# A decoder trunk in FP32: the depth of the weight splits in the first 20 blocks, vector prices in the planner, a margin for woven steps

## The chip, the cores and the metric

One core of a Trainium2 chip runs one launch. The metric is the device time of that launch in microseconds (us). Five engines work side by side: TensorE (PE in the profile; its weight loads are listed apart as PEld), VectorE (DVE), ScalarE (ACT), GpSimd (POOL) and SyncE (SP), which issues most DMAs. About 0.2% of the time is what a measurement of this kernel can tell from no change.

## What is computed

Two layers act on 512 prompt tokens and 8 x 4 sample tokens, 544 columns in all, in FP32. Each layer is a mixer (a retention part and a dilated attention part that read one projection) and a ConvFFN:

```python
x += W_out [ RetentionGroup(h) || DilatedAttnGroup(h) ],  h = RMSNorm(x)   # h @ W_in, 28 column blocks of 128
x += ConvFFN(RMSNorm(x))                # up-proj -> causal conv width 3 -> SiLU gate -> down-proj
```

The attention of the prompt is, for each head and each strip of 128 queries, `p = exp(s - m)`, `den = sum(p)`, `o = (p / den) @ v`. A final RMSNorm ends the trunk.

## The kernel before

**Products.** Each FP32 product is done as three FP32R products: a weight tile `raw` is split into a rounded part `wh` (ACT, a copy) and the rest `wl` (DVE, `raw - wh`; for `w_up` ACT and a GpSimd DMA that adds). The activations are split likewise into `xh` and `xl`. A main block is one column block of 128 outputs: for each of its 8 `k` (128 rows of the contraction) it issues 6 matmuls of 272 columns (3 products, 2 halves of the tokens) into a PSUM tile `ps`. These 6 are called a k-step here. Two `ps` tiles exist, so a block may start when the block before the last one has been read out (its "evacuation").

**Weight units.** `halves` lists the units of weights in the order of use; the blocks 0 and 1 have two units each (s = 0 to 3), then each block of `w_in` and `w_up` has one. `load_w(s)` issues the DMA of unit s on SP, `split_w(s)` issues `wh` on ACT at once and puts `wl` into the planner's list under the name "split". There are RAWS = 3 raw tiles and UNITS = 4 pairs of `wh` and `wl`. In the loop at line 1428 the block that uses unit s loads unit s + 4 when it starts and splits unit s + 3 in its middle.

**The start.** Blocks 0 and 1 run together (lines 1406 to 1423) before the first RMSNorm is known. The norm's sum of squares goes through PE into `sec`, then ACT and DVE make `rstd` from it (`var`, two `tmp`, `rstd` on DVE). Block 0's `ps` is copied to `ev` by ACT, and `va` on DVE is `ev` or `ps` times `rstd`. Block 3 can't start before block 1's `ps` has been read by its `va`. GpSimd multiplies the two rotary tables `rope` by `rstd` as soon as that exists.

**Woven work.** All other work is written as generators: attention units, retention heads, evacuations, splits. `Stream.pump`, called after each k-step, issues from them whatever the planner `Clock` thinks ready. `Clock` holds an estimated end for each tile; `Engine.charge` (line 126) prices each instruction. The order in which instructions stand in each engine's queue is set when the program is built, by these estimates alone; on the chip each queue runs in that order and waits on semaphores. A PE piece is issued when its inputs are estimated done MARGIN = 0.3 us before PE's estimated time.

**An attention unit** (`att_unit`, line 735) has two halves: scores on PE (`sec<-ka,qa`), bias and maximum on DVE (`p<-sec,cst`), exponential and sum on ACT, then on DVE a reciprocal of one column and a scale of the whole tile (`tensor_scalar`, in the profile `TENSOR_SCALAR p<-p,pm`, of 128 to 512 columns), then the transposes on PE (`sec<-cst,p`). There are 32 such halves in each layer's first 16 blocks, where the blocks' evacuations (`rotary_out`: `ra`, four `rb` on DVE, then two additions `ka` or `qa` on GpSimd) fall as well.

**Woven down-projection** (`Weave`). The first 16 of the 22 ConvFFN rows go through `w_down` in 4 groups by a scheme with 7 products where 8 would be needed. A group has 4 sets m of 7 steps (P1, P4, P6, P2, P5, P7, P3), 6 matmuls each into `sec`, put between the k-steps of the next group's blocks. `tick` counts k-steps: a step is issued when it is `ready`, or at the latest when the count forces it (line 622). The weights of a set are split into `ah`, `al` (DVE) and the sums `sh`, `sl` (DVE); P1 and P4 are the first to use `al`.

Of the kernel before, what the change touches and what calls it, by code (L numbers as in the profile page):

```python
# [27 lines left out]
STEPS = (("P1", 0, 0), ("P4", 0, 2), ("P6", 1, 1), ("P2", 0, 1), ("P5", 1, 0), ("P7", 1, 2), ("P3", 1, 3))  # L28

LEAD, AMONG = 24, 40  # L30
EPS = 1e-6
NEG = -1e30
BLK = 562
# [13 lines left out]
NCONV = 352  # L47
EARLY = 640
RAWS, UNITS = 3, 4


def ADDED(block):
# [52 lines left out]
class Engine:  # L105
# [20 lines left out]
    def charge(self, method, outs, ins, args, kw):  # L126
        c, kind = self.clock, self.kind
        n = free_size(outs[0]) if outs else 0
        if method == "dma_start" and kind == "pool":
            c.issue(kind, [], [*outs, *ins], 1.0)  # L130
            c.dma = max(c.dma, c.now["pool"] + 1.0) + n * outs[0].shape[0] * 4 / 1.8e5
            c.wrote[c.key(outs[0])] = ("sp", c.dma + 1.0)
            return
        if method == "dma_start":
            c.now["sp"] = max(c.now["sp"], c.when("sp", ins)) + 0.06
            c.dma = max(c.dma, c.now["sp"] + 0.8) + n * outs[0].shape[0] * 4 / 3.6e5
            c.wrote[c.key(outs[0])] = ("sp", c.dma + 1.0)
            return
        if kind == "pe":
            rows = outs[0].shape[0]  # L140
            if method == "transpose":
                cost = max(n, 128) * 2 / 2400
            elif (kw["lhsT"]).dtype == F32R:
                cost = max(n / 2400, 0.107)
            else:
                side = min(rows, kw["lhsT"].shape[0])
                cost = max(n * 4 / 2400, 0.21) / (1 if side > 64 else 128 // side)
            cost += 0.003
        elif kind == "act":
            ptr = sum(free_size(i) == 1 for i in ins[1:])  # L150
            cost = 1.3 if method.startswith("preload") else n / 1200 + 0.093 * (1 + ptr)
        elif kind == "dve":
            half = method in ("tensor_scalar", "tensor_copy")
            cost = (n * (0.5 if half else 1) + 66 + (60 if len(ins) > 2 else 0)) / 960
        else:
            cost = 0.1 + n * (2.2 if len(ins) > 1 else 1.0) / 1000
        c.issue(kind, outs, ins, cost)
# [84 lines left out]
def trunk(ctx: ExitStack, tc: tile.TileContext, xin, w_in, w_out, w_up, w_down, q_down, kc, vc, s0, sctx_d, params_d,  # L242
          consts_d, rope_d, y_o, kv_o, pret_o, sret_o, conv_o):
    nc = tc.nc
    clock = Clock()
    pe, act, dve, pool, sp = (Engine(clock, k, e) for k, e in (
        ("pe", nc.tensor), ("act", nc.scalar), ("dve", nc.vector), ("pool", nc.gpsimd), ("sp", nc.sync)))
# [59 lines left out]
    def done(n=1):  # L307
        st.banks += n
# [31 lines left out]
    def load_w(s):  # L340
        if s < len(halves):
            i, a, b = halves[s]
            if s < 4:
                raw[s] = blk([128, b - a, 128], F32, "raw")
            else:
                raw[s] = rotate(wpool.tile([128, b - a, 128], F32, name=name("raw"), tag="raw", bufs=RAWS), "raw",
                                RAWS)
            sp.dma_start(*weights_of(s, raw[s]))
# [52 lines left out]
    class Norm:  # L401
# [47 lines left out]
        def rsqrt(self, ps, shape):  # L449
# [6 lines left out]
            for c, p in enumerate(ps):  # L456
                dve.tensor_scalar(v[:, c], p[:, :HC], -0.5 / D, -0.5 * EPS, op0=OP.mult, op1=OP.add)
            done(len(ps))
# [142 lines left out]
    class Weave:  # L601
# [25 lines left out]
        def ready(self, m, p, g, q):  # L627
            if (m, g) not in self.weights or any(p not in self.forms(i) for i in range(self.nk)):
                return False
            aps = [*self.weights[m, g], *(t for i in range(self.nk) for t in self.forms(i)[p])]  # L630
            return clock.when("pe", aps) <= clock.now["pe"]

        def prepare(self):

# [771 lines left out]
    for k in range(KB):  # L1406
        if k == 2:
            load_w(5)
        if k == 4:
            split_w(4)  # L1410
            load_w(6)
        if k == 6:
            split_w(5)
            load_w(7)
        for n in range(2):
            s = 2 * n + k // 4
            products(main[n], ps[n], k, parts_of(s), k // 4 * 4)
            if k % 4 == 3:
                split.pop(s)
            if k == KB - 1:  # L1420
                main[n]["evac"](ps[n])
                ps[n] = None
            st.pump(0.7)
    sp.dma_start(cst[1], consts_d[:, EARLY:])
    sp.dma_start(taps, params_d[:, NPAR:])

    split_w(6)
    for i, b in enumerate(main[2:-KB]):
        st.block = i + 2
        if b["pre"]:  # L1430
            b["pre"]()
        ps = main_bank()
        for pi, (a, e) in enumerate(b["parts"]):
            s = b["first"] + pi
            at, count = b["at"], b["count"]
            if at == 0:
                load_w(s + 4)
                w = parts_of(s)
                split.pop(s)
            for k in range(a, e):  # L1440
                if 2 * (at * (e - a) + k - a) == count * (e - a):
                    split_w(s + 3)
                products(b, ps, k, w, a - at * (e - a))
                st.pump(0.7)
                if b["weave"]:
                    b["weave"].tick()
        b["evac"](ps)
        st.pump()
# [3 lines left out]
    for c in range(2):  # L1452
        for n, b in enumerate(main[-KB:]):
            s, nk = b["first"], b["nk"]
# [145 lines left out]
```

## Time and profile before

| what | value |
|---|---|
| time, median of 3 runs | 1438.18 us (1438.09 to 1438.63) |
| the profiled execution | 1439.3 us |
| its span, first to last instruction | 1437.5 us |
| mean granted TensorE clock | 0.993 |
| PE busy | 1407.0 us, 98% of the span |
| DVE, ACT, POOL busy | 68%, 46%, 32% |

The span is what the trace covers; 1.8 us of the profiled execution lie around it. Since PE is busy for 98% of the span, the views of interest are those that show PE's stops: the waits by engine, the timeline around a stop, and the stretches with the granted clock. A matmul's end is modelled, and matmuls overlap, so the distance from start to start of two matmuls tells more than their durations. All calls go through one helper, so every row has line L123, and the tiles' names tell the groups apart.

### The profile page before, as it was taken

Reading aid. Unit: us, or ns where it says so; the run is one execution under the profiler, and the core shown is the slowest. Engines: PE = TensorE matmul, PEld = TensorE weight load, DVE = VectorE, ACT = ScalarE, POOL = GpSimd, SP = SyncE. Lnnn points to the kernel's source line nnn. Section 1 sums busy time; section 2 is a strip of 40 time slices with the busy share of each in tenths; the row PEclk is TensorE's granted clock in tenths of the full one; section 3 lists DMA queues with packets and bytes.
Section 4 is the critical chain, followed back from the end, with each engine's and each line's share of the span. In section 5 each row is a group of like instructions: output and inputs, shape, how many; then the busy total and the mean of one; then the engine's idle time right before and its main releaser. Section 6 shows DMA issues by size and latency. Waiting matters only on the chain.

```text
span 1437.5 us, 28709 instructions
## 1 busy us (share of the span) xinstructions
PE 1407.0 (98%) x11442; PEld 1336.1 (93%) x11442; DVE 977.5 (68%) x1823; ACT 667.3 (46%) x1074; POOL 457.8 (32%) x833
## 2 busy tenths in 40 slices
PE   8999999999999999999999999999999999999997
PEld 7888878999999999999997888889999999999996
DVE  8767545576577777776777764455856786868665
ACT  5254223436555454554434452233666454645434
POOL 4312211102546455541022231110135464645303
PEclk8999999999999999999999999999999999999999
DMA  6224584348765656563331247733677566566522
GB/s 252 75 83 156 187 318 157 125 132 212 180 170 129 172 132 171 125 174 82 102 132 69 87 158 269 286 122 117 201 174 179 155 139 164 131 174 143 138 71 77
DMA packets 83494, 219.99 MB, mean 153 GB/s; under 512 B 8992, under 2 KB 13216, under 8 KB 83360
## 3 DMA queue, kind: packets, MB, share of 16 engines
q1 hardware_dynamic: 70688, 172.01, 34.7%
q0 software_dynamic: 12672, 46.14, 18.3%
q8 instruction: 90, 1.47, 0.4%
q14 instruction: 44, 0.36, 0.1%
HBM read 205.91 MB, written 12.21 MB: 152 GB/s over the span
## 4 chain that ended last, share of the span: by engine, by line
PE 81%; DVE 10%; POOL 4%; issue 3%; ACT 2%; DMA 0%; SPq 0%; DVEq 0%; ACTq 0%; POOLq 0%
PE ps L123 58%; PE sec L123 23%; DVE p L123 3%; DVE rb L123 2%; POOL fb L123 1%; POOL fa L123 1%; POOL sums L123 1%; DVE wl L123 1%; DVE c L123 1%; DVE ra L123 1%; ACT fh L123 1%; DVE lb L123 0%; DVE x L123 0%; ACT wh L123 0%; DVE al L123 0%
## 5 line engine op out<-in xcount | busy, mean ns | idle before, releaser
L123 PE MATMUL ps<-xh,wh 128*128 128x272 f32 x2304 | 491.1, 295 | 4.4 <-DVE va L123 3.5
L123 PE MATMUL ps<-xh,wl 128*128 128x272 f32 x2304 | 478.4, 289 | 1.5 <-DVE wl L123 1.4
L123 PE MATMUL ps<-xl,wh 128*128 128x272 f32 x2304 | 478.3, 289 | 0.0
L123 PEld LDWEIGHTS ps<-xh,wh 128*128 128x128 f32 x2304 | 361.6, 189 | 22.2 <-issue 19.2
L123 PEld LDWEIGHTS ps<-xh,wl 128*128 128x128 f32 x2304 | 363.0, 189 | 1.9 <-DVE wl L123 1.9
L123 PEld LDWEIGHTS ps<-xl,wh 128*128 128x128 f32 x2304 | 363.1, 189 | 0.1
L123 ACT ACTIVATE wh<-raw 128x1024 fp32r<-128x1024 f32 (+1 forms) x182 | 181.9, 1000 | 66.9 <-PE ps L123 54.6
L123 ACT ACTIVATE c<-u,taps 128x560 f32<-128x560 f32 x88 | 75.4, 857 | 238.4 <-DVE u L123 200.0
L123 POOL DMA_DIRECT2D wl<-w_up x88 | 76.8, 873 | 336.4 <-ACT wl L123 314.4
L123 DVE SCALAR_TENSOR_TENSOR c<-u,taps,c 128x560 f32<-128x560 f32 x176 | 150.6, 856 | 45.4 <-ACT c L123 41.9
L123 DVE TENSOR_TENSOR x<-x,sec 128x272 f32<-128x272 f32 (+1 forms) x224 | 105.9, 475 | 91.4 <-PE sec L123 89.8
L123 DVE TENSOR_TENSOR wl<-raw,wh 128x1024 fp32r<-128x1024 f32 (+1 forms) x94 | 108.0, 1151 | 13.7 <-ACT wh L123 11.1
L123 POOL COPY last<-u 128x2 f32<-128x2 f32 (+1 forms) x176 | 39.2, 260 | 176.2 <-DVE u L123 176.2
L123 ACT ACTIVATE wl<-wh 128x1024 fp32r<-128x1024 f32 x88 | 92.7, 1053 | 1.3
L123 DVE TENSOR_TENSOR u<-ps,rstd 128x512 f32<-128x512 f32 (+1 forms) x176 | 68.9, 433 | 35.0 <-PE ps L123 34.7
L123 DVE TENSOR_TENSOR rb<-ps,rope 32x544 f32<-32x544 f32 (+1 forms) x96 | 69.2, 721 | 1.4
L123 DVE TENSOR_TENSOR x<-x,ps 128x544 f32<-128x544 f32 (+1 forms) x72 | 46.9, 654 | 31.0 <-PE ps L123 30.9
L123 POOL TENSOR_TENSOR sums<-uraw 128x256 f32<-128x256 f32 x64 | 63.6, 995 | 10.2 <-DVE sl L123 10.2
L123 DVE CUSTOM_DVE_ANT_0 p<-sec,cst 128x128 f32<-128x128 f32 (+3 forms) x64 | 29.2, 489 | 53.1 <-PE sec L123 52.8
L123 POOL TENSOR_TENSOR kr<-ra,rb 128x512 f32<-128x512 f32 (+1 forms) x16 | 14.2, 911 | 151.0 <-DVE rb L123 69.4
L123 PE MATMUL sec<-fh,sl 128*128 128x272 f32 x192 | 55.4, 289 | 0.3 <-DVE sl L123 0.3
L123 PE MATMUL sec<-fl,sh 128*128 128x272 f32 x192 | 55.3, 288 | 0.0
(196 smaller groups left out, 2537.3 us busy)
## 6 DMA issues: line engine op xcount, KB each, us to landing
raw<-w_up SPq DMA_DIRECT2D x88, 512.0 KB, 4.5
wl<-w_up POOLq DMA_DIRECT2D x88, 512.0 KB, 5.6
raw<-w_in SPq DMA_DIRECT2D x54, 512.0 KB, 4.1
kt<-kc SPq DMA_DIRECT2D x80, 256.0 KB, 5.9
vt<-vc SPq DMA_DIRECT2D x80, 256.0 KB, 5.0
uraw<-q_down SPq DMA_DIRECT2D x32, 512.0 KB, 4.1
raw<-w_out SPq DMA_DIRECT2D x16, 512.0 KB, 3.7
s<-s SPq DMA_DIRECT2D x16, 256.0 KB, 6.0
```

Of the source, the lines that this page charges most:

```text
L123: return f(*args, **kw)
```

## The change

Three edits. In `charge`, DVE's `tensor_scalar` and `tensor_copy` are priced by all their columns, not half of them, and `tensor_scalar` and `reciprocal` get 0.09 us more. In `Weave.ready` a woven step counts as ready only when its operands are estimated done LATE = 1.0 us before PE's time (line 631). In the block loop the split goes two units ahead and the load three, up to block index i = 20, where both catch up by one unit (two loads and two splits in that block); the load of unit 7 in the opening loop and the split of unit 6 behind it fall away, since the loop does them now.

```diff
@@ -28,6 +28,8 @@
 STEPS = (("P1", 0, 0), ("P4", 0, 2), ("P6", 1, 1), ("P2", 0, 1), ("P5", 1, 0), ("P7", 1, 2), ("P3", 1, 3))
 
 LEAD, AMONG = 24, 40
+
+LATE = 1.0
 EPS = 1e-6
 NEG = -1e30
 BLK = 562
@@ -47,6 +49,7 @@
 NCONV = 352
 EARLY = 640
 RAWS, UNITS = 3, 4
+DEEPER = 20
 
 
 def ADDED(block):
@@ -150,8 +153,9 @@
             ptr = sum(free_size(i) == 1 for i in ins[1:])
             cost = 1.3 if method.startswith("preload") else n / 1200 + 0.093 * (1 + ptr)
         elif kind == "dve":
-            half = method in ("tensor_scalar", "tensor_copy")
-            cost = (n * (0.5 if half else 1) + 66 + (60 if len(ins) > 2 else 0)) / 960
+            cost = (n + 66 + (60 if len(ins) > 2 else 0)) / 960
+            if method in ("tensor_scalar", "reciprocal"):
+                cost += 0.09
         else:
             cost = 0.1 + n * (2.2 if len(ins) > 1 else 1.0) / 1000
         c.issue(kind, outs, ins, cost)
@@ -628,7 +632,7 @@
             if (m, g) not in self.weights or any(p not in self.forms(i) for i in range(self.nk)):
                 return False
             aps = [*self.weights[m, g], *(t for i in range(self.nk) for t in self.forms(i)[p])]
-            return clock.when("pe", aps) <= clock.now["pe"]
+            return clock.when("pe", aps) + LATE <= clock.now["pe"]
 
         def prepare(self):
 
@@ -1411,7 +1415,6 @@
             load_w(6)
         if k == 6:
             split_w(5)
-            load_w(7)
         for n in range(2):
             s = 2 * n + k // 4
             products(main[n], ps[n], k, parts_of(s), k // 4 * 4)
@@ -1424,7 +1427,7 @@
     sp.dma_start(cst[1], consts_d[:, EARLY:])
     sp.dma_start(taps, params_d[:, NPAR:])
 
-    split_w(6)
+    ahead = 2
     for i, b in enumerate(main[2:-KB]):
         st.block = i + 2
         if b["pre"]:
@@ -1434,12 +1437,17 @@
             s = b["first"] + pi
             at, count = b["at"], b["count"]
             if at == 0:
-                load_w(s + 4)
+                load_w(s + ahead + 1)
+                if i == DEEPER:
+                    ahead = 3
+                    load_w(s + ahead + 1)
                 w = parts_of(s)
                 split.pop(s)
             for k in range(a, e):
                 if 2 * (at * (e - a) + k - a) == count * (e - a):
-                    split_w(s + 3)
+                    if i == DEEPER:
+                        split_w(s + ahead - 1)
+                    split_w(s + ahead)
                 products(b, ps, k, w, a - at * (e - a))
                 st.pump(0.7)
                 if b["weave"]:
```

What the edits move, at three places. The numbers in the names are buffer numbers, which count differently in the two programs; the changed program's helper stands at line 126.

DVE at the start, from the estimate `tmp` of the first norm to the evacuation of block 1 (`va` from `ps_198`); `wl` are splits of weight units. Before:

```order
L123 TENSOR_TENSOR tmp_310<-rstd_308 128x544
L123 TENSOR_TENSOR tmp_310<-tmp_310,var_309 128x544
L123 TENSOR_TENSOR wl_326<-raw_252,wh_325 128x1024
L123 SCALAR_TENSOR_TENSOR rstd_308<-tmp_310,rstd_308 128x544
L123 TENSOR_TENSOR wl_360<-raw_281,wh_359 128x1024
L123 TENSOR_TENSOR va_377<-ev_302,rstd_308 128x512
L123 TENSOR_TENSOR va_377<-ev_302,rstd_308 128x32
L123 TENSOR_TENSOR va_380<-ps_198,rstd_308 128x512
L123 TENSOR_TENSOR va_380<-ps_198,rstd_308 128x32
```

And in the changed program:

```order
L126 TENSOR_TENSOR tmp_308<-rstd_306 128x544
L126 TENSOR_TENSOR tmp_308<-tmp_308,var_307 128x544
L126 SCALAR_TENSOR_TENSOR rstd_306<-tmp_308,rstd_306 128x544
L126 TENSOR_TENSOR va_364<-ev_300,rstd_306 128x512
L126 TENSOR_TENSOR va_364<-ev_300,rstd_306 128x32
L126 TENSOR_TENSOR va_367<-ps_198,rstd_306 128x512
L126 TENSOR_TENSOR va_367<-ps_198,rstd_306 128x32
L126 TENSOR_TENSOR wl_354<-raw_252,wh_353 128x1024
L126 TENSOR_TENSOR ra_392<-ps_323,rope_187 128x544
```

The two `wl` that stood before and behind `rstd` are gone from there: unit 6's stands behind the evacuation, unit 7's comes a block later.

DVE in layer 0, one attention unit of 256 columns (`p` from `sec` is the bias step, TENSOR_SCALAR the scale) and the evacuation of block 5 (`ra`, `rb`). Before:

```order
L123 ISA p_641,pm_642<-sec_637,cst_81 128x256
L123 ISA pm_642 128x1
L123 ISA p_644,pm_645<-sec_639,cst_81 128x256
L123 ISA pm_645 128x1
L123 TENSOR_TENSOR ra_648<-ps_567,rope_187 128x544
L123 TENSOR_TENSOR rb_649<-ps_567,rope_189 32x544 x4
L123 RECIPROCAL pm_642<-pm_642 128x1
L123 TENSOR_SCALAR p_641<-p_641,pm_642 128x256
L123 RECIPROCAL pm_645<-pm_645 128x1
L123 TENSOR_SCALAR p_644<-p_644,pm_645 128x256
```

And in the changed program:

```order
L126 TENSOR_TENSOR ra_624<-ps_561,rope_187 128x544
L126 TENSOR_TENSOR rb_625<-ps_561,rope_189 32x544 x4
L126 ISA p_679,pm_680<-sec_675,cst_81 128x256
L126 ISA pm_680 128x1
L126 ISA p_682,pm_683<-sec_677,cst_81 128x256
L126 ISA pm_683 128x1
L126 RECIPROCAL pm_680<-pm_680 128x1
L126 TENSOR_SCALAR p_679<-p_679,pm_680 128x256
L126 RECIPROCAL pm_683<-pm_683 128x1
L126 TENSOR_SCALAR p_682<-p_682,pm_683 128x256
```

The unit's scales stood right behind `rb` and now stand behind both bias steps, which follow `rb`.

PE at the first woven step of layer 0's second group (`sec` from `h`, `l` and `al`), among the k-steps of a block (`ps_5693`). Before:

```order
L123 MATMUL ps_5693<-xh_3762,wh_5481 128x272 x2
L123 MATMUL ps_5693<-xl_3777,wh_5481 128x272 x2
L123 MATMUL ps_5693<-xh_3762,wl_5482 128x272 x2
L123 MATMUL sec_5712<-h_883_5425,ah_5671 128x272
L123 MATMUL sec_5712<-l_884_5426,ah_5671 128x272
L123 MATMUL sec_5712<-h_883_5425,al_5672 128x272
```

And in the changed program:

```order
L126 MATMUL ps_5693<-xh_3762,wh_5481 128x272 x2
L126 MATMUL ps_5693<-xl_3777,wh_5481 128x272 x2
L126 MATMUL ps_5693<-xh_3762,wl_5482 128x272 x2
L126 MATMUL ps_5693<-xh_3820,wh_5481 128x272 x2
L126 MATMUL ps_5693<-xl_3834,wh_5481 128x272 x2
L126 MATMUL ps_5693<-xh_3820,wl_5482 128x272 x2
L126 MATMUL ps_5693<-xh_3850,wh_5481 128x272 x2
L126 MATMUL ps_5693<-xl_3861,wh_5481 128x272 x2
L126 MATMUL ps_5693<-xh_3850,wl_5482 128x272 x2
L126 MATMUL sec_5727<-h_883_5425,ah_5671 128x272
L126 MATMUL sec_5727<-l_884_5426,ah_5671 128x272
L126 MATMUL sec_5727<-h_883_5425,al_5672 128x272
```

The step stands two k-steps later; the first steps of the other three groups move by two, four and two k-steps in the same way, in both layers, and the last step of each group stays where it was.

## Rows read from the trace of the kernel before

**Rows 1.** The page: busy us (share of the span) xinstructions, engine by engine.

```profile
PE 1407.0 (98%) x11442; PEld 1336.1 (93%) x11442; DVE 977.5 (68%) x1823; ACT 667.3 (46%) x1074; POOL 457.8 (32%) x833
```

**Rows 2.** Waits of PE: waiter <- releaser: us in total, times, longest us.

```profile
PE sec L123 <- DVE p L123: 6.8, 8, 1.1
PE ps L123 <- DVE va L123: 3.5, 1, 3.5
PE sec L123 <- DVE al L123: 3.0, 6, 0.6
...
PE sec L123 <- DVE sl L123: 0.3, 2, 0.2
```

**Rows 3.** Waits of PE's weight loads, same columns.

```profile
PEld sec L123 <- DVE p L123: 6.9, 14, 1.0
```

**Rows 4.** Timeline at the start: start us, us, engine line op out<-in xcount [idle before].

```profile
27.19 1.22 DVE L123 TENSOR_TENSOR wl<-raw,wh 128x1024 fp32r<-128x1024 f32 x1
...
28.33 0.72 DVE L123 SCALAR_TENSOR_TENSOR rstd<-tmp,rstd 128x544 f32<-128x544 f32 x1
...
28.96 1.22 DVE L123 TENSOR_TENSOR wl<-raw,wh 128x1024 fp32r<-128x1024 f32 x1
...
29.18 3.93 POOL L123 TENSOR_TENSOR rope<-rope,rstd 128x544 f32<-128x544 f32 x2 [12.27 <-ACT wh L123]
...
30.10 3.06 DVE L123 TENSOR_TENSOR va<-ev,rstd 128x512 f32<-128x512 f32 x2
30.12 0.41 PE L123 MATMUL ps<-xh,wl 128*128 128x272 f32 x2
...
33.09 0.78 DVE L123 TENSOR_TENSOR va<-ps,rstd 128x512 f32<-128x512 f32 x2
...
34.01 0.79 PE L123 MATMUL ps<-xh,wh 128*128 128x272 f32 x2 [3.48 <-DVE va L123]
...
39.54 0.41 PE L123 MATMUL ps<-xh,wh 128*128 128x272 f32 x2
```

**Rows 5.** Stretches: us, busy us (x) of PE PEld DVE ACT POOL, PEclk, DMA, GB/s.

```profile
5.30:8.80 3.50, 2.29 (x12) 1.54 (x11) 2.55 (x4) 2.30 (x5) 2.17 (x2) 0.99 0.98 302
8.80:15.60 6.80, 5.57 (x24) 5.57 (x25) 6.80 (x5) 6.25 (x11) 6.64 (x5) 0.50 1.03 406
...
29.20:32.60 3.40, 1.33 (x11) 1.11 (x9) 3.40 (x3) 1.06 (x1) 3.40 (x2) 1.00 0.75 294
32.60:39.50 6.90, 5.49 (x24) 5.53 (x25) 6.00 (x9) 0.00 (x0) 2.51 (x2) 0.51 0.22 82
39.50:60.00 20.50, 19.10 (x151) 17.90 (x150) 13.11 (x25) 5.04 (x14) 6.24 (x10) 1.00 0.34 116
```

**Rows 6.** Timeline of an attention unit: the scales of its two halves.

```profile
63.36 1.53 POOL L123 TENSOR_TENSOR qa<-ra,rb 128x512 f32<-128x512 f32 x2 [6.21 <-DVE rb L123]
...
63.45 1.34 DVE L123 TENSOR_SCALAR p<-p,pm 128x256 f32<-128x256 f32 x1
...
64.84 0.90 PE L123 MATMUL sec<-cst,p 128*128 128x128 f32 x4 [0.74 <-DVE p L123]
64.89 0.35 DVE L123 TENSOR_SCALAR p<-p,pm 128x256 f32<-128x256 f32 x1
```

**Rows 7.** Timeline of the unit before it.

```profile
54.52 0.41 PE L123 MATMUL ps<-xh,wl 128*128 128x272 f32 x2
...
56.03 0.30 PE L123 MATMUL sec<-cst,p 128*128 128x128 f32 x1 [1.09 <-DVE p L123]
```

**Rows 8.** Groups by shape: xcount | busy us, mean ns | idle before.

```profile
L123 DVE TENSOR_SCALAR p<-p,pm 128x512 f32<-128x512 f32 x16 | 13.5, 844 | 0.6
```

**Rows 9.** Timeline at the first woven step of layer 0's second group.

```profile
468.84 0.29 PE L123 MATMUL sec<-l,ah 128*128 128x272 f32 x1
...
469.68 0.39 PE L123 MATMUL sec<-h,al 128*128 128x272 f32 x1 [0.56 <-DVE al L123]
```

**Rows 10.** Chain of waits, a long unbroken piece: start us, us, what.

```profile
335.86 65.33 PE ps L123 x522
```

## The prediction, made before the changed kernel ran

> **What bounds the kernel now.** The page comes first: PE is busy for 1407.0 of 1437.5 us, no other engine for more than 977.5 [rows 1]. So the end moves only by what PE stops for, and an edit that changes no product can win no more than PE's stops. The waits of PE name them [rows 2]: 6.8 us in 8 stops for `p` from DVE (the scaled probabilities that attention transposes), 3.5 us in one stop for `va`, 3.0 us in 6 stops for `al` (the first woven steps), 0.3 us in 2 for `sl`. The weight loads add short waits of their own for `p`, 14 in all [rows 3]. These four are what the edits can reach. Each begins on DVE, so the timeline around each stop tells what DVE did just before.
>
> PE's cost of a k-step comes from a piece of the chain without a break: 522 matmuls in 65.33 us, 0.125 us each, 0.75 us for a k-step of six and 6.0 us for a block [rows 10]. A stop costs a little more than PE's idle time: from 54.52 to 56.03 us two matmuls (0.25 us) and a stop pass, so the stop is 1.26 us where the wait is put down as 1.09 [rows 7]; likewise 0.84 - 0.13 = 0.71 for a wait of 0.56 [rows 9]. I add 0.16 us to each.
>
> **The start.** Block 3 waits for block 1's `va`. DVE's chain to it is rows of one kind each [rows 4]: `wl` 1.22, `rstd` 0.72, `wl` 1.22, `va` from `ev` (two instructions) 3.06, `va` from `ps` 0.78, and PE goes on 0.14 us behind that, at 34.01. PE's last matmuls before it start at 30.12 and would have been followed at 30.37, so the stop costs 3.64 us. The change takes both `wl` out of this chain; nothing else stands in it. `rstd` then starts at about 27.3, where the first `wl` started at 27.19 behind `tmp`, and ends at 28.0. How long `va` from `ev` takes then is not in the trace. It lasted 3.06 because GpSimd's two `rope` products ran beside it: they took 3.93 with the waits, and with `va` to the end of 33.16 the two engines took turns. GpSimd's and DVE's work between 30.18 (the end of `wl`) and 33.16 is 2.98 us, of which `va` itself is about 0.78 (the same two shapes from `ps`), so one `rope` product is about 1.1. With `rstd` done at 28.0 DVE is first: `va` (0.6), one `rope` product (1.1), the small second `va` (0.2), 1.9 together; then `va` from `ps` until 30.7, and PE at 30.85. The stop shrinks from 3.64 to about 0.5: **3.1 us won**. Bounds: if `va` is as slow as before the shift is 30.10 - 28.05 = 2.05 us; if no `rope` product comes between, the stop goes altogether, 3.64. I take 3.1, since turns are what the row shows. Next late is nothing near: block 4 needs the `wl` of unit 6, which now ends at about 30.7 + 1.2 = 31.9, while block 3 keeps PE until 30.85 + 6.0 = 36.9. Load 7 leaves SP one block later and its split with it, one DMA of 512 KB, one `wh` and one `wl`; the constants behind it on SP move ahead of it, and no row of PE's waits names a DMA.
>
> The clock adds to this. From 32.6 to 39.5 us it was granted at 0.51, the 1.2 GHz level, right behind the stop, and at 2.4 GHz again from then on [rows 5]. From 34.01 to 39.54 twelve pairs of matmuls took 5.53 us [rows 4], at 0.25 a pair they take 3.01: **2.5 us lost**. Would it fall behind a stop of 0.5 us? The stretch from 39.5 to 60.0 holds the stop of 1.26 and stays at 1.00. Against that, the clock also fell at 8.8 us, and PE was busy for 2.29 of the 3.5 us before, in which no single stop was as long as 3.48 [rows 5]. A stop of 0.5 us is nearer to the first kind, so I count 2.5 as won, and zero as the bound.
>
> **Splits two ahead in the other blocks.** Each block's split is one `wh` and one `wl` of 1.22 us, as many as before; only the block in which they are issued is one later. With the margin of 5.0 us at block 4 (36.9 - 31.9), the tightest, the products of a block hide them; if DVE fell more than 5 us behind, PE would wait for each. At block index 22 two units are split in one block, 2.4 us of DVE under 6.0 us of PE. Cost nothing.
>
> **The prices of DVE.** The scale of 512 columns was priced (256 + 66) / 960 = 0.34 us and is now 0.69; it takes 0.84 in the mean [rows 8]. The row hides two kinds. Of one unit's two scales of 256 columns one took 0.35 and one 1.34 us, the latter starting 0.09 us after GpSimd's `qa` addition of 1.53, and PE waited 0.74 for it [rows 6]. So a collision with GpSimd costs about 1.0 us, and it comes where a scale stands right behind the `rb` that releases GpSimd. The new prices put the transposes of a half 0.25 to 0.45 us later (0.16 + 0.09 at 128 columns, 0.36 + 0.09 at 512), twice that for the second half, and they reorder DVE: in the order, the 256-column unit shown above had its scales right behind `rb`, and now has both bias steps and the exponential between. Going through the 32 halves of a layer in this way, eight scales stood where `rb` or another long GpSimd piece had just begun; about three stand so now. What can be won is PE's stops for `p`: 6.8 + 8 x 0.16 = 8.1 us by PE's rows, and 6 more short ones that only the weight loads show [rows 3], at 0.16 each 1.0, so 9.1 for both layers. Three eighths of it stay with the remaining collisions, 3.4, and the rest goes: **5.7 us won**. Bounds: 0 (the collisions move, and PE's stops with them) and 9.1. More, but smaller, pieces of transposes on PE cost little: no instruction is added.
>
> This is where a rule speaks against the edit. The Trainium skill, page "SBUF — State Buffer", section "SBUF: two separate sides", says that VectorE and GpSimd share a pair of ports as an exclusive lock, and that the loser blocks fully until the other's instruction ends. The pair of 0.35 and 1.34 us agrees with that [rows 6]. By that rule the price of a scale depends on GpSimd's queue and not on its columns, and a flat price would leave the attention's stops as they are: the sum would be without the 5.7.
>
> **The margin of woven steps.** In the groups 1 to 3 (of 0 to 3) of each layer the first step (P1) stops for `al`: 3.0 us in 6 stops [rows 2], with 0.16 each 4.0 us; group 0 has none. In the order P1 now stands two to four k-steps later, 1.5 to 3.0 us of PE's work, against a stop of about 0.7 [rows 9]. In group 2 `al` itself comes behind two evacuation pairs more, some 1.6 us at the 0.78 of such a pair [rows 4], and there P1 moves by four. All six go: 4.0 won. What is lost: in six places of the 8 groups two steps (P3 of one set, P6 of the next) between which `sl` is made anew stand three k-steps apart instead of four or five. The two waits for `sl` of before lie at such a distance, 0.3 us in 2 [rows 2], 0.3 each with the addition. I count half of 6 x 0.3: 0.9. Steps that the count forces are issued without asking; the last step of a group is where it was. **3.1 us won**, bounds 0.9 (each place stops, 1.8, and two stops for `al` stay, 1.3) and 4.0.
>
> **Sum.** 3.1 + 2.5 + 5.7 + 3.1 = 14.4 us. The profiled execution would go from 1439.3 to 1424.9, its span from 1437.5 to 1423.1. The median of the runs stands 1.1 us under the profiled execution; I take the sum off that median: 1438.2 - 14.4 = **1423.8 us**.
>
> **Rivals.**
> 1. *The attention's stops move and stay.* Scales still meet GpSimd, only other ones, and PE stands at their transposes as before. For it: collisions are set by GpSimd's queue [rows 6], and a flat price can't see them; against it: in the order fewer scales stand behind `rb`. Without the 5.7: 1438.2 - 8.7 = 1429.5. The rule of the port lock leads here.
> 2. *The start gives only the shift.* `va` stays slow, the stop is 1.6 us and the clock falls all the same, as it did at 8.8: 1438.2 - 2.05 - 5.7 - 3.1 = 1427.4.
> 3. *Forced steps stop.* With the first steps later the rest is pushed against the deadline and stops there for `sl` and `al` as much as was won: 1438.2 - 11.3 = 1426.9.
> 4. *No change.* The new order in attention has as many stops again, another 8.1 us on top of the old ones: 1438.2 - 8.7 + 8.1 = 1437.6. Gaps of three k-steps between scores and transposes are common in the new order; against it, they were in the old one too, and most had no stop.
> 5. *Slower: units come late.* One block of lead is gone. If DVE, 68% busy, falls behind in the attention blocks by more than the 5 us of margin, each of 18 blocks waits for its `wl`, at 1.22 us [rows 4]: + 22, so 1438.2 - 14.4 + 22 = 1445.8. It decides at a margin of zero; PE's waits before name `wl` nowhere near these blocks.
>
> **Chances.** Forecast 0.45, rival 1 0.27, rival 2 0.10, rival 3 0.06, rival 4 0.07, rival 5 0.05. Faster by over 0.2% (under 1435.3; 0.2% is about what a measurement here can tell from no change) holds in the forecast and rivals 1 to 3: 0.88; within 0.2% 0.07; slower 0.05. The lower end has all bounds at their best: 3.64 + 2.5 + 9.1 + 4.0 = 19.2, so 1419. The upper end takes rival 1 with the clock's 2.5 not won, 1432.0. Rivals 4 and 5 and a little of the tails are left out.
>
> **What would show it.** At the start: no stretch at 0.5 behind 16 us, no `wl` between `tmp` and `va`, and PE's wait for `va` under 1 us. In attention: PE's waits for `p` at 2 to 3.5 us in place of 6.8, and the scales' mean at 512 columns under 0.8. In the ConvFFN: no wait for `al` at a first step, waits for `sl` under 1.5 us. The prediction fails if PE's waits for `p` are as long as before (rival 1), if the clock still falls near 32 us, or if `wl` shows among PE's waits in the first 20 blocks.

## The result, and the profile after

The changed kernel takes 1419.1 us in the median of 4 runs (1418.8 to 1419.9) beside 1438.4 for the kernel before: a ratio of 0.9863, 95% interval 0.9848 to 0.9879. That is 19.3 us, where the prediction had 14.4, and 1438.2 x 0.9863 = 1418.5 lies just under the low end of its range. The sign was right, and one term was too small.

The page of the profiled execution (1419.2 us, its span 1417.4), as in [rows 1]:

```profile
PE 1400.1 (99%) x11442; PEld 1332.8 (94%) x11442; DVE 965.2 (68%) x1823; ACT 668.8 (47%) x1074; POOL 437.7 (31%) x833
```

The longest waits of PE (us in total, times, longest), to be read against [rows 2]:

```profile
PE ps L126 <- DVE wl L126: 3.0, 2, 2.0
PE sec L126 <- DVE eps L126: 1.1, 1, 1.1
PE sec L126 <- DVE x L126: 0.8, 3, 0.4
PE sec L126 <- POOL qa L126: 0.7, 2, 0.4
PE ps L126 <- ACT yh L126: 0.5, 2, 0.3
PE ps L126 <- DVE va L126: 0.3, 1, 0.3
```

The waits for `p` (6.8 us) and `al` (3.0 us) are gone altogether, the one for `va` is 0.3 in place of 3.5. The two waits for `wl` lie at 6 to 11 us, before any edit acts. No stop of over 0.6 us is left behind that.

At the start (start us, us), against [rows 4]:

```profile
27.09 0.72 DVE L126 SCALAR_TENSOR_TENSOR rstd<-tmp,rstd 128x544 f32<-128x544 f32 x1
...
27.85 1.96 DVE L126 TENSOR_TENSOR va<-ev,rstd 128x512 f32<-128x512 f32 x2
...
27.96 3.12 POOL L126 TENSOR_TENSOR rope<-rope,rstd 128x544 f32<-128x544 f32 x2 [11.83 <-ACT wh L126]
...
29.73 0.78 DVE L126 TENSOR_TENSOR va<-ps,rstd 128x512 f32<-128x512 f32 x2
...
30.43 1.72 DVE L126 TENSOR_TENSOR wl<-raw,wh 128x1024 fp32r<-128x1024 f32 x1
...
30.65 0.49 PE L126 MATMUL ps<-xh,wh 128*128 128x272 f32 x2 [0.30 <-DVE va L126]
```

No `wl` stands between `rstd` and `va`; `va` from `ev` takes 1.96 us (forecast 1.9, before 3.06), and PE goes on at 30.65 (forecast 30.85, before 34.01). The clock in the stretches of [rows 5] that matter (us, busy us of PE, PEld, DVE, ACT, POOL, then PEclk):

```profile
8.80:15.60 6.80, 4.88 (x26) 4.88 (x27) 6.80 (x5) 6.38 (x11) 6.64 (x5) 0.75 1.04 409
...
32.60:39.50 6.90, 6.90 (x58) 6.89 (x57) 6.74 (x10) 1.69 (x3) 2.76 (x3) 1.00 0.22 83
```

Behind the short stop PE ran at 2.4 GHz (1.00); before, this stretch had 0.51.

Where the time went is read from the starts of main blocks, each being 48 matmuls into `ps`. Block 4 starts at 43.02 before and 37.22 after, block 44 (behind layer 0's attention) at 380.00 and 368.65, block 74 at 636.40 and 623.46, block 130 (behind layer 1's attention) at 1082.96 and 1064.10. The columns below are cut at these four blocks and bear the name of what the edits touch in them. By differences, in us won of the profiled executions, for the changed kernel and those of the next section:

| kernel | start, to block 4 | attention, layer 0 | ConvFFN, layer 0 | attention, layer 1 | the rest | sum |
|---|---|---|---|---|---|---|
| forecast | 5.6 | 2.85 | 1.55 | 2.85 | 1.55 | 14.4 |
| changed kernel | 5.8 | 5.6 | 1.6 | 5.9 | 1.3 | 20.2 |
| prices alone | 1.2 | 5.6 | 0.2 | 5.8 | 0.3 | 13.2 |
| depth alone | 5.6 | 0.0 | -0.1 | 0.4 | 0.4 | 6.2 |
| margin alone | -0.2 | 0.0 | 2.1 | 0.5 | 1.8 | 4.3 |
| room 0.5 | 2.6 | 2.7 | 0.1 | 3.2 | 0.2 | 8.8 |
| room 1.2 | 0.9 | 6.0 | 0.0 | 6.4 | 0.4 | 13.6 |
| GpSimd short, order of before | 4.7 | 4.3 | 0.4 | 5.1 | 0.5 | 15.0 |
| GpSimd short, changed order | 6.4 | 6.2 | 2.0 | 6.2 | 2.3 | 23.1 |

Start and ConvFFN came out as forecast. Attention gave 11.5 us in place of 5.7, and that is the whole miss. Some columns hold more than the edits. The start holds what the clock gave or took in that one execution: prices, margin and room leave the program ahead of block 4 as it was, and their starts read -0.2 to 2.6 (last section). The two ConvFFN columns (layer 0's and the rest) also vary: three more variants of the changed kernel whose PE runs the same instructions in the same order there (`DEEPER = 2` and the two with room, below) won 1.9 to 2.3 and 2.3 to 2.5 where the changed kernel won 1.6 and 1.3.

### The profile page after: what moved, and what is told of

The parts are those of the page before. It is cut to its first block, busy times and chain, and to the rows that moved or that the text cites. A ratio compares the mean times of both kernels' runs of the same rounds, so it can differ in the third digit from the quotient of the medians.

```text
span 1417.4 us, 28714 instructions
## 1 busy us (share of the span) xinstructions
PE 1400.1 (99%) x11442; PEld 1332.8 (94%) x11442; DVE 965.2 (68%) x1823; ACT 668.8 (47%) x1074; POOL 437.7 (31%) x833
## 4 chain that ended last, share of the span: by engine, by line
PE 91%; DVE 3%; DMA 2%; POOL 2%; issue 1%; ACT 0%; DVEq 0%; SPq 0%; POOLq 0%; ACTq 0%
PE ps L126 69%; PE sec L126 22%; DMA uraw<-q_down 2%; POOL sums L126 1%; DVE rb L126 1%; DVE wl L126 1%; DVE x L126 0%; DVE c L126 0%; POOL qa L126 0%; DMA x<-xin 0%; ACT c L126 0%; DVE tmp L126 0%; DVE va L126 0%; POOL wl L126 0%; DVEq L1594 0%
## 5 line engine op out<-in xcount | busy, mean ns | idle before, releaser
L126 POOL TENSOR_TENSOR sums<-uraw 128x256 f32<-128x256 f32 x64 | 56.4, 881 | 57.9 <-DVE sl L126 39.8
L126 PE MATMUL sec<-fh,sh 128*128 128x272 f32 x192 | 55.4, 289 | 0.0
```

What stands on the lines that cost most here:

```text
L126: return f(*args, **kw)
```

## The experiments

**Each edit by itself.** The three kernels are the one before with one part of the change.

Prices alone:

```diff
-            half = method in ("tensor_scalar", "tensor_copy")
-            cost = (n * (0.5 if half else 1) + 66 + (60 if len(ins) > 2 else 0)) / 960
+            cost = (n + 66 + (60 if len(ins) > 2 else 0)) / 960
+            if method in ("tensor_scalar", "reciprocal"):
+                cost += 0.09
```

> The kernel before with the new prices of DVE alone. Measured for all three edits together: the attention stages became shorter by about 11.0 us (block 4 to block 20 of layer 0 by 5.4, the same blocks of layer 1 by 5.6), where I had summed 5.7. Theory A (room): the prices alone do this, since the planner now puts a half's transposes later than its scale, and the collisions that are left fall into that room: 1438.4 - 11.0 = 1427.4. Rival (depth): the blocks with splits two ahead shifted the wl among DVE's work in attention, and that earned the other half: then the prices alone give my 5.7, 1432.7. Under both the start keeps its stop of 3.6 us for va with 2.5 of half clock, and the six stops for al stay.

Measured: 1426.3 us, ratio 0.9917 (0.9901 to 0.9934): 12.1 us. The table's attention is 5.6 and 5.8. So the prices do all of it, and the rival (depth) falls.

Depth alone (the changed kernel without the hunks on prices and margin):

```diff
-    split_w(6)
+    ahead = 2
...
-                load_w(s + 4)
+                load_w(s + ahead + 1)
...
-                    split_w(s + 3)
+                    split_w(s + ahead)
```

> The kernel before with splits two ahead in the first 20 blocks alone. Theory A: 3.3 us from the shorter stop for va and 2.5 from the clock, nothing in attention or ConvFFN: 1438.4 - 5.8 = 1432.6, with 16 scales still lengthened beside GpSimd. Rival (depth): another 5.3 us in the attention of layer 0 alone, 1427.3, and nothing in layer 1, which lies behind the first 20 blocks.

Measured: 1433.3 us, ratio 0.9963 (0.9948 to 0.9978): 5.2 us. Its waits of PE show the first row at its old length, and `va` gone:

```profile
PE sec L126 <- DVE p L126: 6.8, 8, 1.1
PE sec L126 <- DVE al L126: 3.1, 6, 0.6
...
PE ps L126 <- DVE va L126: 0.3, 1, 0.3
```

Margin alone:

```diff
-            return clock.when("pe", aps) <= clock.now["pe"]
+            return clock.when("pe", aps) + 1.0 <= clock.now["pe"]
```

> The kernel before with the margin of woven steps alone. Theory A: 1.5 us in each layer's ConvFFN, 3.0 together, 1438.4 - 3.0 = 1435.4: the six stops for al (4.0 us) go and about 1.0 of new stops comes, for sl or sh at later steps. Rival (the margin pays only with the rest): the ConvFFN gets new stops as long as the old ones, 1438.4. The first 250 us of each layer are as before.

Measured: 1435.6 us, ratio 0.9977 (0.9967 to 0.9988): 2.8 us. The three gains add up to 20.1 us against 19.3 for the changed kernel; the edits hardly touch each other.

**Why the prices gave twice the forecast: room or fewer collisions?** A collision is a scale that runs beside a GpSimd instruction and is lengthened by it; room is how far behind a scale's estimated end the planner lets its transposes in. A scale counts as lengthened here where its row is over 0.15 us longer than the shortest of its shape. Before there are 16 of 64, 8 in each layer, and PE has 22 distances from start to start ahead of transposes that are longer than the usual one behind a matmul of the same kind and shape, 12.0 us together. (The expectations below have 12.4, which comes out if 0.2 us behind each of two score products `sec<-ka,qa` of 384 columns is counted as a stop; 0.41 us is the ordinary distance behind these, in every kernel here.) With the change 6 scales are lengthened, 3 in each layer, as forecast, and no longer distance is left. So the collisions that stay cost PE next to nothing. The scales by shape in the changed kernel (xcount | busy us, mean ns), the first against [rows 8]:

```profile
L126 DVE TENSOR_SCALAR p<-p,pm 128x512 f32<-128x512 f32 x16 | 10.9, 682 | 0.6
L126 DVE TENSOR_SCALAR p<-p,pm 128x384 f32<-128x384 f32 x16 | 6.7, 421 | 0.6
```

A collision that stayed, at 76 us of the same trace:

```profile
75.97 1.69 POOL L126 TENSOR_TENSOR ka<-ra,rb 128x512 f32<-128x512 f32 x2 [18.92 <-DVE rb L126]
...
76.03 1.52 DVE L126 TENSOR_SCALAR p<-p,pm 128x512 f32<-128x512 f32 x1
...
77.65 0.49 DVE L126 TENSOR_SCALAR p<-p,pm 128x512 f32<-128x512 f32 x1
...
78.02 1.03 PE L126 MATMUL sec<-cst,p 128*128 128x128 f32 x8
```

Of two scales of one shape the one beside GpSimd takes 1.52, the other 0.49. In [rows 6] and [rows 7] PE stood still at this point; here its transposes come at 78.02, 0.48 us behind the first scale, with no wait in the row, after products that filled the time. Over all 64 halves the transposes start, in the median, about 1.3 us behind the end of their own scale, before about 0.2. For the six lengthened scales it is 0.06 (twice), 0.47, 0.48, 1.99 and 2.27; the two at 0.06 cost PE at most 0.05 us each.

That could be room alone, so the old prices got room by itself:

```diff
+ROOM = 0.5
...
+        if kind == "pe+":
+            return max(self.clock.when("pe", aps) + ROOM, self.bank_free(banks)) + MARGIN <= now
...
-            yield PE(pr[s], banks=1)
+            yield need("pe+", pr[s], banks=1)
```

> The kernel before with its old prices, but the transposes of the scaled probabilities are let in 0.5 us later than the planner's estimate of their scale (one number in the test of readiness). Theory A (room): PE's stops ahead of transposes in attention, 12.4 us start to start for both layers before, fall under 3, although about as many scales (12 to 20 of 64) are still lengthened beside GpSimd: 1438.4 - 10 = 1428.4. Rival B (order): what the new prices won came from fewer collisions, 6 instead of 16; room without new prices leaves the collisions and their stops of about 1 us, and only the short stops behind undisturbed scales go, about 2 us: 1436.4.

Measured: 1431.9 us, ratio 0.9954 (0.9939 to 0.9969), between the two. 14 scales are lengthened, and 10 of them still have their transposes right behind, within 0.15 us:

```profile
L123 DVE TENSOR_SCALAR p<-p,pm 128x512 f32<-128x512 f32 x16 | 16.1, 1005 | 0.6
```

```profile
PE sec L123 <- DVE p L123: 2.1, 6, 0.6
...
PE sec L123 <- POOL qa L123: 1.2, 4, 0.3
```

The stops ahead of transposes fall from 12.0 to about 3.1 us (the next expectation has 4.0, counted as the 12.4), and attention wins 5.9. Room of 0.5 is less than the 1.0 by which a collision lengthens a scale. With 1.2:

```diff
-ROOM = 0.5
+ROOM = 1.2
```

> As the room of 0.5 us, with 1.2 us, more than a collision lengthens a scale (1.0). With 0.5 us, 14 scales stayed lengthened, the stops ahead of transposes fell from 12.4 to 4.0 us and attention became 5.5 us shorter. Theory A (room is enough where it is larger than the collision): 12 or more scales lengthened, stops ahead of transposes under 1.5 us, attention 9 to 11 us shorter: 1428. Rival B (the new prices won by fewer collisions as much as by room): the stops ahead of transposes go, but transposes so late make others wait (pt, qa, the next unit's scores), so attention wins 5 to 7 us as with 0.5: 1432.

Measured: 1425.6 us, ratio 0.9915 (0.9899 to 0.9932), attention 12.4 us shorter, the old prices notwithstanding. Eight scales are lengthened, by 8.3 us together, and not one has a transpose waiting behind it; PE's waits have no row for `p`:

```profile
L123 DVE TENSOR_SCALAR p<-p,pm 128x512 f32<-128x512 f32 x16 | 12.0, 748 | 0.6
L123 DVE TENSOR_SCALAR p<-p,pm 128x384 f32<-128x384 f32 x16 | 8.7, 545 | 0.6
```

Theory A holds where the room exceeds the collision. Room also moved the collisions from 14 to 8, so with 1.2 it isn't the only thing that changed; that the 8 cost nothing is what the run shows.

The other way round, the collisions were taken out and the order kept. GpSimd's additions of the rotation and its `rope` products work on 8 columns, while the planner goes on charging them in full. The result lacks the second half of the rotations.

```diff
-        pool.tensor_add(two(dst[:, 0:SEQ], PC), a[:, :, 0:PC], b[:, :, 0:PC])
-        pool.tensor_add(two(dst[:, SEQ:NT], SC), a[:, :, PC:HC], b[:, :, PC:HC])
+        f, e = (t.rearrange("p c n -> p (c n)") for t in (a, b))
+        for lo, hi, n in ((0, SEQ, PC), (SEQ, NT, SC)):
+            pool.charge("tensor_add", [f[:, lo:hi]], [f[:, lo:hi], e[:, lo:hi]], (), {})
+            nc.gpsimd.tensor_add(f[:, lo:lo + 8], f[:, lo:lo + 8], e[:, lo:lo + 8])
...
-            pool.tensor_mul(t, t, norm.rstd)
+            pool.charge("tensor_mul", [t], [t, norm.rstd], (), {})
+            nc.gpsimd.tensor_mul(t[:, :, :8], t[:, :, :8], norm.rstd[:, :, :8])
```

> The kernel before in its own order (the planner still charges GpSimd's additions and rope products in full), but on the chip each of these works on 8 columns in place of 272 or 256: the rotations' second half is left out of the result. Theory: a scale is lengthened by the GpSimd instruction beside it. Then at most 2 to 4 of 64 scales stay lengthened (beside qd, which is not shortened), and of PE's stops ahead of transposes (12.4 us) about 10 go, the 2 behind undisturbed scales stay; at the start va from ev takes about 0.8 instead of 3.06, 2.2 more: 1438.4 - 12 = 1426. Rival: the lengthening has another cause (ACT, PSUM, the waits of DVE itself): 12 or more scales stay long, 1436 to 1438.

Measured: 1424.2 us, ratio 0.9904 (0.9889 to 0.9919). Four scales of 512 columns stay long, all beside GpSimd instructions that were not shortened: two beside `qd`, two beside a memset. The unit of [rows 6] now reads:

```profile
57.33 0.50 POOL L545 TENSOR_TENSOR ra<-ra,rb 128x8 f32<-128x8 f32 x2 [6.28 <-DVE rb L123]
57.42 0.35 DVE L123 TENSOR_SCALAR p<-p,pm 128x256 f32<-128x256 f32 x1
...
57.88 0.37 DVE L123 TENSOR_SCALAR p<-p,pm 128x256 f32<-128x256 f32 x1
...
57.92 0.27 PE L123 MATMUL sec<-cst,p 128*128 128x128 f32 x1
```

In the same place and order the first scale takes 0.35 instead of 1.34, and PE doesn't wait for it. Attention wins 9.4 us, and 4.4 of the 12.0 are left. The collisions with GpSimd were the larger part of what attention lost.

The same edit in the changed kernel:

> The changed kernel in its own order, with GpSimd's additions and rope products on 8 columns (the rotations' second half is left out of the result). In the kernel before this took 8.8 us out of attention. Theory (room): of the 6 scales still lengthened in the changed kernel 4 become short, and PE hardly notices, as its transposes stand 1.28 us behind their scale in the middle of the list instead of 0.23: attention within 0.6 us, and up to 0.5 us at the start, 1418.1 to 1419.1. Rival (my forecast's step): a collision that is left costs a stop as before, 3.4 us in all: 1415.7.

Measured: 1416.2 us, ratio 0.9844 (0.9830 to 0.9859). No scale is long any more:

```profile
L126 DVE TENSOR_SCALAR p<-p,pm 128x512 f32<-128x512 f32 x16 | 7.8, 489 | 0.6
```

The time is near the rival's 1415.7, but not by the rival's way. Attention wins 0.9 us over the changed kernel, and that is no more than its two stops for GpSimd's own `qa`, which go (0.7 in 2 above, 1.0 from start to start). The rest, 0.6 at the start and 1.4 from the ConvFFN stages to the end, lies where no scale stands. The 1.4 can't be put down to the shorter GpSimd work: the three variants named under the table, with GpSimd's work in full, won 1.5 to 1.7 there over the same execution of the changed kernel, and their stops at woven steps are 0.8 us where this run has 1.3 and the changed kernel 1.9. What differs between these executions stays open.

**The start: how much of one `wl`?** One of the two `wl` is put back into the chain:

```diff
+    split_w(6)
     ahead = 2
...
-                    split_w(s + ahead)
+                    if i:
+                        split_w(s + ahead)
```

> The changed kernel, but the split of unit 6 stands ahead of block 2 as before, and the one at block 2's middle is dropped: one wl of 1.22 us (and a little more beside GpSimd) is back in DVE's chain to va. Theory: PE's stop for va goes from 0.47 us (start to start) to 1.7, and the time by as much: 1419.1 + 1.2 = 1420.3, with the clock at 2.4 GHz behind the stop. Rival: the fall of the clock comes with a stop of this length already: another 1.2 to 2.5 us, 1421.5 to 1422.8. In a look at one execution each, the kernel before lost 2.5 us to the clock behind a stop of 3.5 us, the one with new prices alone 1.2 behind the same stop, and the one with room of 0.5 nothing.

Measured: 1419.8 us, ratio 0.9872 (0.9858 to 0.9887), 0.7 above the changed kernel in the median, 1.2 at block 4 in the profiled execution. The timeline and the clock behind the stop:

```profile
27.14 1.22 DVE L126 TENSOR_TENSOR wl<-raw,wh 128x1024 fp32r<-128x1024 f32 x1
...
28.27 0.72 DVE L126 SCALAR_TENSOR_TENSOR rstd<-tmp,rstd 128x544 f32<-128x544 f32 x1
...
31.82 0.49 PE L126 MATMUL ps<-xh,wh 128*128 128x272 f32 x2 [1.30 <-DVE va L126]
```

```profile
32.60:39.50 6.90, 6.90 (x58) 6.89 (x56) 5.17 (x7) 0.93 (x3) 2.75 (x3) 1.00 0.51 159
```

With one `wl` more the stop grows by 1.0 us, from 0.47 to 1.46 start to start, and the clock stays up behind it.

**The depth in the other blocks.**

```diff
-DEEPER = 20
+DEEPER = 2
```

> The changed kernel with splits two ahead only in blocks 2 to 4 (the depth goes back to three at block index 4 in place of 22). Theory: the depth pays at the start alone, the 18 blocks behind it neither win nor lose: the start as in the changed kernel (stop for va 0.5 us), attention within 0.7 us of it, 1419.1. Rival: the lead of three blocks puts a second wl among DVE's work in the blocks of layer 0's attention and makes transposes wait again: 2 to 4 us more in layer 0, 1421 to 1423, with layer 1 unchanged.

Measured: 1419.8 us, ratio 0.9868 (0.9853 to 0.9883); its runs (1418.6 to 1420.2) overlap those of the changed kernel. The profiled execution loses 2.0 us in layer 0's attention, in one place:

```profile
50.43 1.48 POOL L126 TENSOR_TENSOR ka<-ra,rb 128x512 f32<-128x512 f32 x2 [5.94 <-DVE rb L126]
50.49 1.28 DVE L126 TENSOR_SCALAR p<-p,pm 128x128 f32<-128x128 f32 x1
...
51.92 0.69 PE L126 MATMUL sec<-cst,p 128*128 128x128 f32 x2 [1.40 <-DVE pm L126]
```

The rival named this stage for another reason. The same unit in the changed kernel:

```profile
48.65 1.22 DVE L126 TENSOR_TENSOR wl<-raw,wh 128x1024 fp32r<-128x1024 f32 x1
48.79 2.44 POOL L126 TENSOR_TENSOR ka<-ra,rb 128x512 f32<-128x512 f32 x2 [5.00 <-DVE rb L126]
...
49.98 1.11 DVE L126 TENSOR_SCALAR p<-p,pm 128x128 f32<-128x128 f32 x1
...
51.15 0.33 PE L126 MATMUL sec<-cst,p 128*128 128x128 f32 x1
```

There a `wl` stands between the `rb` and the unit's scales, and `ka` begins beside it; the second scale meets `ka` later on and takes 1.11 us, but PE goes on without a stop. With `DEEPER = 2` no `wl` stands there, the first scale meets `ka` at its start, and PE waits 1.40. Both kernels have six lengthened scales. So the depth does act on attention, through the order: it decides which scale of a unit collides, and with how much room.

**Looking for something better.** A larger margin for the woven steps:

```diff
-LATE = 1.0
+LATE = 2.0
```

> The changed kernel with a margin of 2.0 us in place of 1.0 for woven steps. In the changed kernel 6 stops at woven steps are left, 1.9 us start to start, all at the second factor (sh, sl). Theory: 1.0 us covers what DVE is late at al and not all of what it is late at sh: with 2.0 they go, 1419.1 - 1.5 = 1417.6. Rival (forced steps): later steps meet the count that forces them and stop there; no gain or up to 2 us lost, 1419 to 1421.

Measured: 1419.2 us, ratio 0.9869 (0.9855 to 0.9884), no gain; 6 stops of 2.4 us together where there were 6 of 1.9. The largest of these stops in the changed kernel shows why:

```profile
562.71 0.43 DVE L126 TENSOR_TENSOR x<-x,sec 128x272 f32<-128x272 f32 x1
...
563.20 0.39 PE L126 MATMUL sec<-hb,sh 128*128 128x272 f32 x1 [0.40 <-DVE x L126]
```

By the profile's releaser the step waits for DVE's `x`, which reads a finished `sec` out, and not for `sh`. The margin looks at operands alone, so no size of it reaches this.

Room of 1.2 us and the old prices in place of the new ones, depth and margin as changed:

> Splits two ahead and the margin as in the changed kernel, the old prices, and room of 1.2 us for the transposes in place of the new prices. Room alone made attention 12.3 us shorter (layer 0 6.0, layer 1 6.3), the new prices alone 11.3. Theory: the gains add up, 1 us better than the changed kernel: 1418.1. Rival: with the start shifted, other scales meet GpSimd and attention comes out as with the new prices, 1419.

Measured: 1417.2 us, ratio 0.9852 (0.9835 to 0.9868); 1.9 us below the changed kernel in the median, which the intervals don't separate. Its attention (12.1) is 0.6 better; its ConvFFN columns (2.3 and 2.3) are too, by 1.7 us together, but that is the difference which the other variants show as well. So the run doesn't show that room beats the prices. Room on top of the new prices (the other lines of the room edit as above):

```diff
 SLACK = 0.25
+ROOM = 0.7
```

> The changed kernel with room of 0.7 us on top of the new prices. Theory: the stops ahead of transposes are gone already, so more room has nothing to win there: 1419.1, or up to 0.5 us less from waits for qa. Rival: room on top of prices holds back the units, and steps pile up at the end of attention: 1420 to 1422.

Measured: 1421.7 us, ratio 0.9882 (0.9867 to 0.9897), 2.6 us slower than the changed kernel in the median; the runs (1420.8 to 1422.1) lie above that kernel's, while the intervals of the ratios overlap. Attention in layer 1 wins 6.5 us, layer 0 only 0.8. Among the causes are new stops in the sample attention of layer 0, where PE waits for loads of cached values; this is the last of three:

```profile
229.96 1.71 PE L126 MATMUL sec<-vt,pts 128*32 128x512 f32 x4 [0.82 <-DMA vt<-vc]
```

They come to 2.0 us of the 4.7 missing; the rest wasn't traced.

## Why the prediction was right and wrong

**The start was right in mechanism and size.** Stop 3.64 to 0.47 us, 3.2 won for a forecast of 3.1; `va` from `ev` 1.96 for an estimate of 1.9 from engines that take turns. The clock term came out as well, but with luck: 2.5 us is what the one profiled execution had lost, and of four others with the same program up to there three lost less (last section).

**Splits elsewhere cost nothing:** right for depth alone (0.0 in layer 0's attention). What I had not seen is that a `wl` more or less between `rb` and a scale decides which scale collides, 2.0 us with `DEEPER = 2`.

**The attention term failed,** 5.7 forecast and 11.5 measured, in two places of its working.
1. The step "Three eighths of it stay with the remaining collisions, 3.4". The count was right: eight collisions in a layer before, three after. But I let a collision that stays cost PE as much as before, though the sentence ahead of it said that transposes come 0.25 to 0.45 us later, and twice that for the second half. Room and collisions are one sum: a scale lengthened by 1.0 costs only what exceeds the room. In the runs, room of 0.5 under 14 collisions left about 3.1 us, room of 1.2 left none behind 8, and in the changed kernel the removal of the six that are left won nothing beyond the stops for `qa`. The room was sized too small besides. My figures would not have covered the 0.83 of a second half of 128 columns (twice 0.25), nor the 1.03 of a first half of 512 (0.45); in the trace the transposes of the six start 0.9 to 2.7 us behind where an undisturbed scale would have ended, each time more than its scale was lengthened (0.4 to 1.0). Why the order gave so much more than the prices added isn't shown.
2. The pool of 9.1. Start to start it was 12.0, and all of it went, which fits the 11.5 measured. I had taken PE's rows for `p` and the weight loads' rows for `p`. The same view of PE's waits before has a row that I left out:

```profile
PE sec L123 <- DVE pm L123: 1.3, 4, 0.4
```

`pm` is the reciprocal's tile, and these four are stops ahead of transposes too. With 0.16 each that is 1.9 of the 2.9 that lacked.

With the right pool and my three eighths the term is 7.5, with my pool and nothing staying 9.1; only both together come near 11.5. My lower bound took the pool for the most that could be won, so the range was cut at the same wrong number.

**The port rule.** The row of a scale at 0.35 where it had 1.34, once GpSimd worked on 8 columns, agrees with what the Trainium skill says on the page "SBUF — State Buffer", section "SBUF: two separate sides": VectorE and GpSimd hold a shared pair of ports in turn, and the loser waits for the whole instruction. I had concluded that by this rule a flat price leaves the stops as they are (rival 1). The rule held in this row and the conclusion was wrong: the price can't foresee the collision, but it moves the transposes behind it.

**The margin was right in size, wrong in what it lost.** The six stops for `al` (4.0) went. I expected 0.9 lost to waits for `sl`; the two for `sl` became shorter (0.7 to 0.4), and 1.5 came at four steps, three of which the rows put down to `x`, the reading out of a `sec` (0.8 us in 3 above). Net 2.9 in the table for a forecast of 3.1.

**Rivals 2 to 5 fell:** the clock stayed up, also behind the 1.5 us of the run with one split in the chain; no woven step stopped for `al`, and those for `sl` lost 0.4 us in all; attention won; and PE's waits name no `wl` behind the first 11 us.

## What to carry to other kernels

Size a pool of stops by the distances from start to start at the waiting instruction, against the usual distance behind the same kind and shape of matmul, whatever name the wait is put down to: the rows for `p` alone gave 9.1 where the distances give 12.0. Where an edit gives a consumer more distance, set that distance against each delay that remains, one by one, before letting a share of the loss stay. A planner that can't foresee a collision can still be made safe by room larger than it, but not by ever more room: on top of the new prices it cost 2.6 us in the median, and 4.7 in layer 0's attention. Before a microsecond in a stage is put down to an edit, see what other runs with the same instructions there take.

## What the runs showed that I had not expected

Behind the same stop of about 3.5 us for `va`, the clock fell for a different share of the time from kernel to kernel, though nothing differs in the program up to there: 0.51 from 32.6 to 39.5 us in the kernel before [rows 5], and in three others:

```profile
32.60:39.50 6.90, 5.52 (x24) 5.55 (x25) 5.97 (x9) 0.00 (x0) 2.51 (x2) 0.53 0.22 82
```

```profile
32.60:39.50 6.90, 5.55 (x34) 5.58 (x35) 5.94 (x9) 0.00 (x0) 2.51 (x2) 0.75 0.22 82
```

```profile
32.60:39.50 6.90, 5.65 (x45) 5.68 (x46) 5.84 (x9) 0.00 (x0) 2.50 (x2) 1.00 0.23 84
```

The first is the margin alone, the second the prices alone, the third the room of 0.5. The granted clock is at 1.2 GHz for nearly all, about half or none of the stretch, and block 4 starts 2.7 and 1.4 us later in the first two than in the third. In each of the five executions with this stop the value is within 0.01 of that of the stretch from 8.8 to 15.6 us (0.50, 0.52, 0.75, 0.75 and 1.00). Behind stops of 1.5 us and less it was 1.00 in all nine, also where the earlier stretch had 0.52 to 0.75. So 2.5 us was near the worst of these five executions, and part of the difference between its 6.2 us for the depth and the 5.2 of the medians. The Trainium skill, page "TensorE: Matmul & The Clock Gate", section "Part 1: The HAM clock gate (the "warmup" mystery)", says that the number of slow matmuls at a kernel's start varies from run to run for one kernel. The stretch from 8.8 to 15.6 us agrees, with 0.50 to 1.00; that a later stop behaves so is what the rows above add.

The second surprise is the memset. It reads nothing, and yet the scale beside it took 1.25 us where the other of its unit took 0.49. These rows are of the kernel with short GpSimd work in the order of before:

```profile
91.92 1.25 DVE L123 TENSOR_SCALAR p<-p,pm 128x512 f32<-128x512 f32 x1
91.94 0.95 POOL L123 MEMSET lent<- 128x1024 f32 x1
...
93.28 0.49 DVE L123 TENSOR_SCALAR p<-p,pm 128x512 f32<-128x512 f32 x1
```

A DVE instruction of two SBUF inputs isn't spared either: at the start `va` from `ev` took 3.06, 1.96 and 0.83 us, by what `rope` product of GpSimd stood beside it (0.83 with the products on 8 columns).
